# Weights split once, keys transposed before they are split: reordering the second half of a projection

## The chip, the cores and the metric

The kernel runs on one core of a Trainium2 chip. Its time is the device time of one execution in microseconds (us), as a median of several runs. TensorE is called PE here, ScalarE ACT, VectorE DVE, GpSimd POOL, and SP is the engine that issues most transfers.

## The reference, cut to what matters

The model is a two-layer encoder of width 1024 on one sequence of 1024 positions: one attention layer, one gated MLP layer, each followed by a dense MLP. Only the start of the first layer is touched by the change: the projection to queries, keys and values.

```python
def gqa_attention(h, w_qkv, q_g, k_g, w_o, cos, sin):
    qkv = h @ w_qkv                                   # 16 query heads, 4 key and 4 value heads of 64
    q, k, v = jnp.split(qkv, [Q_WIDTH, Q_WIDTH + KV_WIDTH], axis=-1)
    q = apply_rope(rmsnorm(q.reshape(B, T, N_HEADS, HEAD_DIM), q_g), cos, sin)
    k = apply_rope(rmsnorm(k.reshape(B, T, N_KV_HEADS, HEAD_DIM), k_g), cos, sin)
    ...
    s = jnp.einsum('bqkgd,bskd->bkgqs', q_blk, k).astype(jnp.float32) * scale
    p = jax.nn.softmax(s, axis=-1).astype(v.dtype)
    return jnp.einsum('bkgqs,bskd->bqkgd', p, v)
```

Everything is float32. The kernel multiplies at the faster rounded type (float32r) and keeps the precision by splitting operands into a rounded high part and the remainder: a product a·b becomes three matmuls, a_hi·b_hi + a_hi·b_lo + a_lo·b_hi. A split is an ACT cast (hi) and a subtraction on DVE or POOL (lo).

## The kernel before

The projection works on two halves of 512 positions. For each half, the normed and modulated input `hs` (second half: `hs1`) is split in 8 tiles of 128 channels. The weights have three column blocks of 512: block 0 holds all keys and values, block 1 the first eight query heads, block 2 the other eight. `qkv_mm(cb, kp, ps, hp)` (L573 to L582) multiplies block `cb` with channel pair `kp`, 24 matmuls into four PSUM banks, one for each 128 positions. A block of one half is four such calls, 96 matmuls.

Weights come through `qkv_w` (L551 to L571): a load of 512 KB into a tile of the tag `c`, two casts, two subtractions. The splits of blocks 0 and 1 stay in memory for both halves. Block 2 is split for the first half, and its tiles are given up; for the second half it is loaded and split again, into tiles of the tags `s` and `w` (`keep=True`).

What is done with the results, in rows of positions:

- `values` splits the values straight out of PSUM. `k_copies` and `q_copies` bring keys and queries from PSUM to memory on ACT.
- `q_sums`, `k_scale`: sums of squares for each head (ACT squares, DVE reduces), a reciprocal root by an ACT square root and one Newton step on DVE, and `qk_scale`, the product with it, on POOL (L654).
- `qk_rope` rotates with the tables (L638 to L641): two products and a sum, on DVE; for the third block of the first half the last sum is POOL's, and its input is read straight out of PSUM.
- `k_split` (L670 to L679) splits the finished keys; each row tile has the four key heads, each head twice side by side.
- `kstacks` (L681 to L689) turns them to channels by positions: for each key head and each of hi and lo, four PE transposes into a bank and one ACT copy into a tile of the tag `x`. A score matmul later takes such a stack, with the same 64 channels in both halves of the partitions, against a query stack with hi above lo.
- `q_stage` splits queries for the attention on POOL, `q_trans` transposes them on PE.

PSUM has eight banks. `banks(True)` gives the four of the pool `ps_s` (two tiles of two banks), `banks(False)` the four of the pool `p_x`; `bank_x` and `bank_s` take one bank-sized tile out of the one or the other. A new tile waits until the oldest one in its place has been read.

The order on each engine comes from a scheduler that works from the order of the code; instructions handed to `pin` or `hold` keep theirs. From the attention on almost all is pinned: its units follow a written order of stages, in which POOL and DVE get further work (`deferred`) at fixed places.

Of the kernel before, what the change touches and what calls it, by code (L numbers as in the profile page):

```python
# [12 lines left out]
F32R = mybir.dt.float32r  # L13
AF = mybir.ActivationFunctionType
ALU = mybir.AluOpType
# [3 lines left out]
P = 128  # L19
# [5 lines left out]
NKV = 4  # L25
HD = 64
EPS = 1e-6
CB = 512
# [8 lines left out]
def encoder_kernel(ctx: ExitStack, tc: tile.TileContext, t: dict, out: bass.AP):  # L37
    nc = tc.nc
    V, S, G, T = nc.vector, nc.scalar, nc.gpsimd, nc.tensor
# [35 lines left out]
    def cwide(dt=F32, shape=(1024,)):  # L75
        return part["pool"].tile([P] + list(shape), dt, tag="c", name=nm("c"), bufs=4)
# [466 lines left out]
    qn = {}  # L543
    kst = {}
# [3 lines left out]
    if True:  # L548
        wq = {}

        def qkv_w(cb, kp, eng, keep=False):  # L551
            raw = qkv_hi(cb, kp, keep)
            for i in range(2):
                qkv_lo(cb, kp, raw, i, eng)
# [14 lines left out]
        def qkv_lo(cb, kp, raw, i, eng):  # L569
            hi, lo = wq[(cb, 2 * kp + i)]  # L570
            hold(eng.tensor_tensor(lo, raw[:, i], f32(hi), ALU.subtract))  # L571

        def qkv_mm(cb, kp, ps, hp, part=(0, 1)):  # L573
            for i in part:
                k = 2 * kp + i
                wh, wl = wq[(cb, k)]
                for j in range(4):
                    hh = hp[k][0][:, j * P : (j + 1) * P]
                    hl = hp[k][1][:, j * P : (j + 1) * P]
                    hold(T.matmul(ps[j], hh, wh, start=k == 0, stop=False))  # L580
                    hold(T.matmul(ps[j], hh, wl, start=False, stop=False))
                    hold(T.matmul(ps[j], hl, wh, start=False, stop=k == KT - 1))  # L582
# [10 lines left out]
        def k_copies(ps):  # L593
            raws = []
            for jj in range(2):
                raw = slot()
                for i in range(2):
                    S.copy(raw[:, i * 256 : (i + 1) * 256], ps[2 * jj + i][:, :256])
                raws.append(raw)
            return raws  # L600

        def q_copies(ps):
            raws = []
            for j in range(4):
                raw = slot()
                S.copy(raw, ps[j])
                raws.append(raw)
            return raws

        def values(hf, ps):  # L610
            for j in range(4):
                v_ = slot(F32R)
                vv = v_.rearrange("p (g s d) -> p g s d", g=NKV, s=2)
                pv = ps[j][:, 256:].rearrange("p (g d) -> p g d", g=NKV)
                S.copy(vv[:, :, 0], pv)
                pin(V.tensor_tensor(vv[:, :, 1], pv, f32(vv[:, :, 0]), ALU.subtract))
# [32 lines left out]
        def q_sums(src):  # L649
            return qk_rstd(qk_sums(src))  # L650
# [5 lines left out]
        def q_rope(hf, cb, src, r, js, add=None):  # L656
            for j in js:
                d = qk_rope(src[j], 0, hf * 4 + j, 1, V, add)
                qk_scale(d, r, j)
                qn[(hf * 4 + j, cb - 1)] = d  # L660

        def k_rows(hf, src):
            return [qk_rope(src[j], 1, hf * 4 + 2 * j, 2) for j in range(2)]

        def k_scale(kd, src):
            r = qk_rstd(qk_sums(src))
            for j in range(2):
                qk_scale(kd[j], r, j)

        def k_split(kd):  # L670
            kk = []
            for j in range(4):
                kh, kl = slot(F32R), slot(F32R)
                src = heads(kd[j // 2], 2)[:, j % 2].unsqueeze(2).broadcast_to([P, NKV, 2, HD])
                hv = kh.rearrange("p (g s d) -> p g s d", g=NKV, s=2)
                S.copy(hv, src)
                V.tensor_tensor(kl.rearrange("p (g s d) -> p g s d", g=NKV, s=2), src, f32(hv), ALU.subtract)
                kk.append((kh, kl))
            return kk  # L679

        def kstacks(hf, kk, bank):  # L681
            for g in range(NKV):
                for s in range(2):
                    pt = bank("kt", dt=F32R)
                    for j in range(4):
                        T.transpose(pt[:, j * P : (j + 1) * P], kk[j][s][:, g * P : (g + 1) * P], identr)
                    d_ = xslot(F32R)
                    S.copy(d_, f32(pt))
                    kst[(g, hf, s)] = d_  # L689

        row = wide("c")
        nc.sync.dma_start(row[0:1, :], t["cond"])
# [1 line left out]
        xs = [load_x(0, k) for k in range(KT)]  # L694
# [14 lines left out]
        sq0, sq1 = SquareSum(), SquareSum()  # L709
# [17 lines left out]
        rb = slot()  # L727
        hs = []
# [60 lines left out]
        pk, pq = banks(True), banks(False)  # L789
# [5 lines left out]
            if k < 6:  # L795
                qkv_mm(1, k // 2, pq, hs, (k % 2,))
        xs1 = [load_x(1, k) for k in range(KT)]
        qkv_w(2, 0, V)
        values(0, pk)
        rk = k_copies(pk)  # L800
        qkv_mm(1, 3, pq, hs, (0,))
        qkv_w(2, 1, V)
        for k in range(2):
            sq1.add(xs1[k])
        tables(*raw_tables)
        qkv_mm(1, 3, pq, hs, (1,))
        ps = banks(True)
        qkv_mm(2, 0, ps, hs)
        r1 = q_copies(pq)
        qkv_w(2, 2, V)  # L810
        for k in range(2, 5):
            sq1.add(xs1[k])
        qkv_mm(2, 1, ps, hs)
        qkv_w(2, 3, V)
        for k in range(5, KT):
            sq1.add(xs1[k])
        qkv_mm(2, 2, ps, hs, (0,))
# [13 lines left out]
        rr2 = q_sums(ps)  # L831
        q_rope(0, 2, ps, rr2, (0, 1), G)
        qkv_mm(0, 1, pk, hs1)
        q_rope(0, 2, ps, rr2, (2, 3), G)
        qkv_mm(0, 2, pk, hs1)
        qkv_w(2, 0, V, True)
        kk = k_split(kd)
        qkv_mm(0, 3, pk, hs1)
        rk = k_copies(pk)
        values(1, pk)  # L840
        pq = banks(True)
        qkv_mm(1, 0, pq, hs1)
# [76 lines left out]


    with ExitStack() as es:

        def q_stage(qq, g):
            qh = []
            for j in range(2):
                q_ = qn[(2 * qq + j, g // 2)]
                src = q_[:, (g % 2) * 256 : (g % 2) * 256 + 256].rearrange("p (h d) -> p h d", h=4)
                d_ = slot(F32R)
                dv = d_.rearrange("p (h s d) -> p h s d", h=4, s=2)
                G.tensor_copy(dv[:, :, 0], src)  # L930
                G.tensor_tensor(dv[:, :, 1], src, f32(dv[:, :, 0]), ALU.subtract)
                qh.append(d_)
            return qh

        def q_trans(qh, hp, qst, bank=bank_x):
            pt = bank("qt", dt=F32R)
# [95 lines left out]
        r2 = q_copies(ps)  # L1032
        rr2 = {}
        r1, rr1 = list(r1), rr
# [18 lines left out]
        del hs, hs1, xs, xs1, rb, rb1, ps, pk, pq, rk, kk, kd, sq0, sq1, wq, r3  # L1053
        for i in range(nu + 2):
            u0 = units[i] if i < nu else None
            u1 = units[i - 1] if 0 < i <= nu else None
# [5 lines left out]
            for op in ORDER.split():  # L1062
                f, w, j = op[0], int(op[1]), int(op[2])
# [402 lines left out]
    for ct in range(24):  # L1466
        i, r = divmod(ct, 3)
# [404 lines left out]
```

## Time and profile before

| | |
|---|---|
| median of 3 runs | 2625.0 us (2622.57 to 2626.14) |
| profiled execution | 2625.42 us |
| its span, first to last instruction | 2623.6 us |
| mean granted TensorE clock | 0.997 |
| PE / DVE / ACT / POOL busy | 99% / 83% / 55% / 28% |
| projection | from the start to about 170 us |
| attention | about 155 to 550 us |
| time from one matmul's start to the next, 128x128 on 512 columns | 0.23 us (one is shown as 0.39: they overlap) |

A row of a timeline has the start, the duration, the engine, the line, the operation with output and inputs (buffer numbers left out), the shape, how many equal ones follow each other (x), and in brackets how long the engine was idle before it and which instruction ended that. Since matmuls overlap, the rate of PE is read from starts, not from durations.

### The profile page before, as it was taken

What the parts mean: (1) busy time and instruction counts of PE and PEld (TensorE: products, weight loads), DVE (VectorE), ACT (ScalarE), POOL (GpSimd) and SP (SyncE); (2) the same over time, 40 slices, a digit from 0 to 9 for tenths busy, and PEclk for the clock granted to TensorE, in tenths of its full rate; (3) what the DMA queues carried; (4) which work ended last, traced back from release to release, by engine and by line L of the source; (5) the groups of instructions that cost most, each with busy time, mean ns of one, the idle gap of its engine ahead of it and who ended that gap; (6) DMA issues with size and microseconds to landing.
All of it is one profiled execution on the core that took longest, in us unless ns stands there. A gap on an engine that the chain in (4) does not pass through costs nothing.

```text
span 2623.6 us, 37299 instructions
## 1 busy us (share of the span) xinstructions
PE 2595.9 (99%) x12856; PEld 2172.3 (83%) x12856; DVE 2185.8 (83%) x3285; ACT 1443.2 (55%) x2588; POOL 722.8 (28%) x531
## 2 busy tenths in 40 slices
PE   9999999999999999999999999999999999999999
PEld 7789999888788888888888888888888788888887
DVE  7868999887989989877897687788989977789974
ACT  4569998854654455445543444445456644465442
POOL 0238776533000004430122054451520000005400
PEclk9999999999999999999999999999999999999999
DMA  8010222234487788644243355568641554487461
GB/s 301 32 33 9 73 85 79 97 100 158 159 287 253 262 312 305 203 126 171 89 153 112 117 183 178 179 208 303 236 143 52 175 178 157 151 314 264 149 213 56
DMA packets 209328, 436.44 MB, mean 166 GB/s; under 512 B 23089, under 2 KB 35505, under 8 KB 209138
## 3 DMA queue, kind: packets, MB, share of 16 engines
q1 hardware_dynamic: 182258, 396.29, 44.8%
q10 hardware_dynamic: 26880, 37.76, 4.0%
q8 instruction: 102, 1.67, 0.3%
q14 instruction: 88, 0.72, 0.1%
HBM read 311.28 MB, written 122.68 MB: 165 GB/s over the span
## 4 chain that ended last, share of the span: by engine, by line
PE 86%; DVE 7%; DMA 3%; ACT 2%; issue 1%; POOL 1%; SPq 0%; DVEq 0%; ACTq 0%
PE w L474 10%; PE w L475 10%; PE w L476 10%; PE out L1218 10%; PE out L1219 10%; PE out L1217 10%; PE s L953 4%; PE o L989 4%; PE t L970 4%; PE v L1576 3%; PE v L1575 3%; PE v L1574 3%; PE mix L1681 2%; DVE t L334 1%; PE qkv L580 1%
## 5 line engine op out<-in xcount | busy, mean ns | idle before, releaser
L1217 PE MATMUL out<-t,s 128*128 128x512 f32 x1232 | 479.5, 390 | 1.2 <-ACT t L333 0.6
L1218 PE MATMUL out<-t,s 128*128 128x512 f32 x1232 | 479.6, 390 | 0.7 <-DVE t L334 0.7
L1219 PE MATMUL out<-t,s 128*128 128x512 f32 x1232 | 479.2, 389 | 0.0
L474 PE MATMUL w<-t,s 128*128 128x512 f32 x1168 | 458.7, 394 | 0.5 <-ACT t L333 0.5
L475 PE MATMUL w<-t,s 128*128 128x512 f32 x1168 | 455.5, 390 | 1.8 <-DVE t L334 1.8
L476 PE MATMUL w<-t,s 128*128 128x512 f32 x1168 | 454.9, 389 | 0.0
L334 DVE TENSOR_TENSOR t<-t,t 128x512 fp32r<-128x512 f32 x408 | 324.2, 805 | 24.4 <-ACT t L333 16.8
L333 ACT CAST t<-t 128x512 fp32r<-128x512 f32 x408 | 245.2, 617 | 120.3 <-DMA t<-hf 70.9
L1217 PEld LDWEIGHTS out<-t,s 128*128 128x128 f32 x1232 | 231.3, 188 | 50.2 <-ACT t L333 1.0
L1218 PEld LDWEIGHTS out<-t,s 128*128 128x128 f32 x1232 | 231.3, 188 | 49.6 <-DVE t L334 1.9
L1219 PEld LDWEIGHTS out<-t,s 128*128 128x128 f32 x1232 | 231.3, 188 | 47.7
L459 ACT CAST s<-w 128x512 fp32r<-128x512 f32 x292 | 173.4, 616 | 164.7 <-PE w L476 107.6
L475 PEld LDWEIGHTS w<-t,s 128*128 128x128 f32 x1168 | 219.5, 188 | 48.7 <-DVE t L334 5.2
L474 PEld LDWEIGHTS w<-t,s 128*128 128x128 f32 x1168 | 219.5, 188 | 47.8 <-issue 2.6
L460 DVE TENSOR_TENSOR s<-w,s 128x512 fp32r<-128x512 f32 x292 | 221.4, 765 | 44.1 <-ACT s L459 43.7
L476 PEld LDWEIGHTS w<-t,s 128*128 128x128 f32 x1168 | 219.4, 188 | 45.4
L1199 ACT CAST s<-t 128x512 fp32r<-128x512 f32 x240 | 148.2, 621 | 193.7 <-PE out L1219 140.2
L1200 DVE TENSOR_TENSOR s<-t,s 128x512 fp32r<-128x512 f32 x240 | 196.7, 821 | 63.1 <-ACT s L1199 62.3
L1185 POOL TENSOR_TENSOR w<-w,t 128x512 f32<-128x512 f32 x20 | 33.4, 1681 | 768.0 <-DMA t<-in_wm_dram 355.1
L956 DVE TENSOR_REDUCE mx<-s 128x1 f32<-128x1024 f32 x128 | 156.3, 1221 | 31.6 <-PE s L953 29.8
L979 DVE TENSOR_TENSOR t<-t,t 128x512 fp32r<-128x512 f32 x256 | 164.2, 682 | 17.8 <-ACT t L973 16.7
L989 PE MATMUL o<-t,t 128*128 128x256 f32 x1024 | 163.5, 293 | 0.0
(253 smaller groups left out, 5081.8 us busy)
## 6 DMA issues: line engine op xcount, KB each, us to landing
t<-hf SPq DMA_DIRECT2D x320, 256.0 KB, 4.1
hf<-c SPq DMA_DIRECT2D x156, 256.0 KB, 3.2
w<-in_wi_dram SPq DMA_DIRECT2D x64, 512.0 KB, 4.2
hf<-c ACTq DMA_DIRECT2D x96, 256.0 KB, 2.3
w<-in_ada_dram SPq DMA_DIRECT2D x36, 512.0 KB, 4.1
x<-in_ada_dram SPq DMA_DIRECT2D x64, 256.0 KB, 5.7
t<-in_wm_dram SPq DMA_DIRECT2D x64, 256.0 KB, 4.8
wf<-w SPq DMA_DIRECT2D x64, 256.0 KB, 2.9
```

What stands on the lines that cost most here:

```text
L333: S.copy(hi, src)
L334: (eng or V).tensor_tensor(lo, src, f32(hi), ALU.subtract)
L459: S.copy(hi, src)
L460: V.tensor_tensor(lo, src, f32(hi), ALU.subtract)
L474: T.matmul(ps, hi[:, a], th, start=kt == 0, stop=False)
L475: T.matmul(ps, hi[:, a], tl, start=False, stop=False)
L476: T.matmul(ps, lo[:, a], th, start=False, stop=kt == 3)
L989: pin(T.matmul(u.po, vt[st][:, u.g * P : (u.g + 1) * P], src[:, s * 256 : (s + 1) * 256], start=st == 0 and part == 0, stop=st == 7 and pa ...
L1200: V.tensor_tensor(lo, src, f32(hi), ALU.subtract)
L1217: T.matmul(ps, hi[:, a], th, start=begin and kt == 0, stop=False, **g)
L1218: T.matmul(ps, hi[:, a], tl, start=False, stop=False, **g)
L1219: T.matmul(ps, lo[:, a], th, start=False, stop=end and kt == 3, **g)
```

## The change

Five things are done, all within the projection.

1. The weights of block 2 are loaded and split once, by a new `qkv_w2`, in loads of 256 KB into tiles of the tag `x`; the high parts stay in tiles `t`, the low parts in tiles `c`, for both halves. The second calls of `qkv_w(2, ...)` are gone.
2. The first queries' copies (`r1`) go to tiles `x` in place of `t`. Third-block queries of the first half are copied out of PSUM by `q_copies` and rotated from there, all on DVE.
3. `k_split` is gone. `kstacks` transposes the scaled keys themselves, two heads at a time (16 transposes in place of 64), and splits them out of PSUM: an ACT cast of one head's 64 partitions, a DVE subtraction for the low part, and an ACT copy of each to the other 64 partitions.
4. The second half's key rows, sums and scale come straight after its key block, the key stacks earlier in the following block; the first key stacks use `bank_s`. The rotations of first and third query block change places.
5. `q_stage(0, 0)` stands in the projection, ahead of the last rotations.

```diff
+        def qkv_w2(kp):
+            lo = wide("c", F32R, (2, CB))
+            for i in range(2):
+                raw, hi = xslot(), slot(F32R)
+                nc.sync.dma_start(raw, t["wqkv"][2, kp][:, i])
+                hold(S.copy(hi, raw))
+                hold(V.tensor_tensor(lo[:, i], raw, f32(hi), ALU.subtract))
+                wq[(2, 2 * kp + i)] = (hi, lo[:, i])
...
-        def k_split(kd):
...
-        def kstacks(hf, kk, bank):
-            for g in range(NKV):
-                for s in range(2):
-                    pt = bank("kt", dt=F32R)
-                    for j in range(4):
-                        T.transpose(pt[:, j * P : (j + 1) * P], kk[j][s][:, g * P : (g + 1) * P], identr)
-                    d_ = xslot(F32R)
-                    S.copy(d_, f32(pt))
-                    kst[(g, hf, s)] = d_
+        def kstacks(hf, kd, bank):
+            for gp in range(2):
+                pt = bank("kt")
+                for j in range(4):
+                    src = kd[j // 2][:, (j % 2) * 256 + gp * P : (j % 2) * 256 + (gp + 1) * P]
+                    T.transpose(pt[:, j * P : (j + 1) * P], src, ident)
+                for i in range(2):
+                    a, b = 64 * i, 64 - 64 * i
+                    hi, lo = xslot(F32R), xslot(F32R)
+                    S.copy(hi[a : a + 64], pt[a : a + 64])
+                    V.tensor_tensor(lo[a : a + 64], pt[a : a + 64], f32(hi[a : a + 64]), ALU.subtract)
+                    S.copy(hi[b : b + 64], f32(hi[a : a + 64]))
+                    S.copy(lo[b : b + 64], f32(lo[a : a + 64]))
+                    kst[(2 * gp + i, hf, 0)], kst[(2 * gp + i, hf, 1)] = hi, lo
...
-        qkv_w(2, 0, V)
+        qkv_w2(0)
         values(0, pk)
         rk = k_copies(pk)
...
-        r1 = q_copies(pq)
-        qkv_w(2, 2, V)
+        r1 = q_copies(pq, xslot)
+        qkv_w2(2)
...
         pk = banks(False)
         qkv_mm(0, 0, pk, hs1)
-        rr2 = q_sums(ps)
-        q_rope(0, 2, ps, rr2, (0, 1), G)
+        r2 = q_copies(ps)
         qkv_mm(0, 1, pk, hs1)
-        q_rope(0, 2, ps, rr2, (2, 3), G)
+        kstacks(0, kd, bank_s)
+        q_rope(0, 1, r1, rr, (0, 1))
         qkv_mm(0, 2, pk, hs1)
-        qkv_w(2, 0, V, True)
-        kk = k_split(kd)
         qkv_mm(0, 3, pk, hs1)
         rk = k_copies(pk)
+        kd = k_rows(1, rk)
+        k_scale(kd, rk)
         values(1, pk)
         pq = banks(True)
         qkv_mm(1, 0, pq, hs1)
-        kd = k_rows(1, rk)
-        qkv_w(2, 1, V, True)
         qkv_mm(1, 1, pq, hs1)
-        kstacks(0, kk, bank_x)
-        k_scale(kd, rk)
-        kk = k_split(kd)
+        q_rope(0, 1, r1, rr, (2, 3))
         qkv_mm(1, 2, pq, hs1)
-        qkv_w(2, 2, V, True)
-        q_rope(0, 1, r1, rr, (0, 1))
+        kstacks(1, kd, bank_x)
+        qh = q_stage(0, 0)
+        rr2 = q_sums(r2)
         qkv_mm(1, 3, pq, hs1)
-        qkv_w(2, 3, V, True)
         r3 = q_copies(pq)
-        kstacks(1, kk, bank_x)
+        q_rope(0, 2, r2, rr2, (0, 1))
         ps = banks(False)
         qkv_mm(2, 0, ps, hs1)
-        q_rope(0, 1, r1, rr, (2, 3))
         rr = q_sums(r3)
+        q_rope(0, 2, r2, rr2, (2, 3))
...
-        qh = q_stage(0, 0)
         nxt = []
         q_trans(qh, 0, nxt, bank_s)
```

How this moves instructions is shown at three places. The first is PE, at the first half's key transposes (`kt`). Before they stood in the middle of the second half's first query block (`qkv_1114` is its last bank), 32 in a row:

```order
L580 MATMUL qkv_1114<-t_292,t_843 128x512
L581 MATMUL qkv_1114<-t_293,t_843 128x512
L582 MATMUL qkv_1114<-t_292,t_845 128x512
L686 MATMUL kt_1183<-identr,t_1055 128x128
L686 MATMUL kt_1183<-identr,t_1059 128x128
L686 MATMUL kt_1183<-identr,t_1063 128x128
L686 MATMUL kt_1183<-identr,t_1067 128x128
L686 MATMUL kt_1190<-identr,t_1056 128x128
```

Now (`t_782` and `t_788` are the key tiles as scaled by POOL, `qkv_925` to `qkv_928` the banks of the second half's key/value block):

```order
L589 MATMUL qkv_925<-w_379,t_859 128x512
L590 MATMUL qkv_925<-w_379,t_859 128x512
L591 MATMUL qkv_925<-w_379,t_861 128x512
L696 MATMUL kt_985<-ident,t_782 128x128 x2
L696 MATMUL kt_985<-ident,t_788 128x128 x2
L589 MATMUL qkv_926<-w_379,t_859 128x512
L590 MATMUL qkv_926<-w_379,t_859 128x512
L696 MATMUL kt_1002<-ident,t_782 128x128 x2
L696 MATMUL kt_1002<-ident,t_788 128x128 x2
L591 MATMUL qkv_926<-w_379,t_861 128x512
```

The eight transposes have moved up into the key/value block, between matmuls of its sixth channel tile (63 matmuls of the block stand ahead of them). Those of the second half have moved likewise, from behind the first query block to a place after 72 of its matmuls.

The second place is ACT at the second half's key stacks. Before, behind the copies of the first queries (`qkv_1113`, `qkv_1114`):

```order
L606 COPY t_1351<-qkv_1113 128x512
L606 COPY t_1353<-qkv_1113 128x512
L606 COPY t_1355<-qkv_1114 128x512
L606 COPY t_1357<-qkv_1114 128x512
L688 CAST x_1364<-kt_1359 128x512
L688 CAST x_1371<-kt_1366 128x512
L688 CAST x_1378<-kt_1373 128x512
L688 CAST x_1385<-kt_1380 128x512
```

Now (L700 is the cast out of PSUM, L702 and L703 the copies of the high and low part to the other partitions):

```order
L700 CAST x_1222<-kt_1217 64x512
L702 CAST x_1222<-x_1222 64x512
L703 CAST x_1223<-x_1223 64x512
L700 CAST x_1228<-kt_1217 64x512
L702 CAST x_1228<-x_1228 64x512
L700 CAST x_1239<-kt_1234 64x512
L703 CAST x_1229<-x_1229 64x512
L702 CAST x_1239<-x_1239 64x512
L703 CAST x_1240<-x_1240 64x512
L700 CAST x_1245<-kt_1234 64x512
L615 COPY t_1303<-qkv_1129 128x512
```

Two banks in place of eight are emptied, each by casts that stand between copies, and DVE's four subtractions (L701, `x_1223`, `x_1229`, `x_1240`, `x_1246`) alternate with them; the copies of the queries come behind. The second of these banks (`kt_1234`) is the one that the last query block's fourth tile, `qkv_1328`, takes over.

The third place is ACT at the first half's values and keys. Before (`qkv_222` and `qkv_223` are key/value tiles of two banks):

```order
L565 CAST t_586<-c_584 128x512
L565 CAST t_589<-c_584 128x512
L615 CAST t_594<-qkv_222 128x4x64
L615 CAST t_597<-qkv_222 128x4x64
L615 CAST t_600<-qkv_223 128x4x64
L615 CAST t_603<-qkv_223 128x4x64
L598 COPY t_606<-qkv_222 128x256 x2
L598 COPY t_609<-qkv_223 128x256 x2
```

Now:

```order
L578 CAST t_586<-x_585 128x512
L578 CAST t_591<-x_590 128x512
L624 CAST t_595<-qkv_222 128x4x64
L624 CAST t_598<-qkv_222 128x4x64
L624 CAST t_601<-qkv_223 128x4x64
L615 COPY x_687<-qkv_224 128x512
L615 COPY x_689<-qkv_225 128x512
L624 CAST t_604<-qkv_223 128x4x64
L607 COPY t_607<-qkv_222 128x256 x2
L615 COPY x_691<-qkv_226 128x512
L607 COPY t_610<-qkv_223 128x256 x2
```

Three copies of first queries (`qkv_224` to `qkv_226`) have moved up among the values' casts and the key copies.

From the attention's first scores on, the order of each engine is what it was.

More of the change, by code (lines that the diff above doesn't have):

```diff
@@ L600, in k_copies, with q_copies @@
             return raws
-        def q_copies(ps):
+        def q_copies(ps, home=slot):
             raws = []
             for j in range(4):
-                raw = slot()
+                raw = home()
                 S.copy(raw, ps[j])
@@ L668, in k_scale, with q_stage @@
                 qk_scale(kd[j], r, j)
-        def k_split(kd):
-            kk = []
-            for j in range(4):
[L673 to L679, printed above, removed]
-        def kstacks(hf, kk, bank):
-            for g in range(NKV):
-                for s in range(2):
-                    pt = bank("kt", dt=F32R)
-                    for j in range(4):
-                        T.transpose(pt[:, j * P : (j + 1) * P], kk[j][s][:, g * P : (g + 1) * P], identr)
-                    d_ = xslot(F32R)
-                    S.copy(d_, f32(pt))
-                    kst[(g, hf, s)] = d_
+        def q_stage(qq, g):
+            qh = []
+            for j in range(2):
+                q_ = qn[(2 * qq + j, g // 2)]
+                src = q_[:, (g % 2) * 256 : (g % 2) * 256 + 256].rearrange("p (h d) -> p h d", h=4)
+                d_ = slot(F32R)
+                dv = d_.rearrange("p (h s d) -> p h s d", h=4, s=2)
+                G.tensor_copy(dv[:, :, 0], src)
+                G.tensor_tensor(dv[:, :, 1], src, f32(dv[:, :, 0]), ALU.subtract)
+                qh.append(d_)
+            return qh
+        def kstacks(hf, kd, bank):
[12 more added lines that the diff above has]
+                    kst[(2 * gp + i, hf, 0)], kst[(2 * gp + i, hf, 1)] = hi, lo
         row = wide("c")
@@ L801, in encoder_kernel @@
         qkv_mm(1, 3, pq, hs, (0,))
-        qkv_w(2, 1, V)
+        qkv_w2(1)
         for k in range(2):
@@ L813, in encoder_kernel @@
         qkv_mm(2, 1, ps, hs)
-        qkv_w(2, 3, V)
+        qkv_w2(3)
         for k in range(5, KT):
@@ L921, in encoder_kernel @@
     with ExitStack() as es:
[L923 to L933, printed above, removed]
         def q_trans(qh, hp, qst, bank=bank_x):
@@ L1052, in encoder_kernel @@
             deferred[3 + 2 * j] = lambda j=j: late_rope(j)
-        del hs, hs1, xs, xs1, rb, rb1, ps, pk, pq, rk, kk, kd, sq0, sq1, wq, r3
+        del hs, hs1, xs, xs1, rb, rb1, ps, pk, pq, rk, kd, sq0, sq1, wq, r3
         for i in range(nu + 2):
```

## Prediction

> **What bounds the kernel now.** I read the page's busy times first, then the waits of the matrix engine (PE) in the stage that changes, then the timelines of PE, ScalarE (ACT), VectorE (DVE) and GpSimd (POOL) there.
>
> ```profile
> PE 2595.9 (99%) x12856; PEld 2172.3 (83%) x12856; DVE 2185.8 (83%) x3285; ACT 1443.2 (55%) x2588; POOL 722.8 (28%) x531
> ```
>
> PE is busy 99% of the span, so only two things shorten this kernel: fewer PE instructions, or fewer PE waits. Here is PE in the projection; columns are start, duration, instruction, and in brackets the idle time before it with what ended it.
>
> ```profile
> 66.83 0.50 PE L580 MATMUL qkv<-t,t 128*128 128x512 f32 x1 [0.85 <-ACT t L598]
> ...
> 89.69 0.39 PE L580 MATMUL qkv<-s,t 128*128 128x512 f32 x1
> ...
> 111.30 0.39 PE L582 MATMUL qkv<-w,t 128*128 128x512 f32 x1
> 113.80 0.47 PE L580 MATMUL qkv<-t,t 128*128 128x512 f32 x1 [2.11 <-DVE t L640]
> ...
> 124.58 0.39 PE L582 MATMUL qkv<-t,t 128*128 128x512 f32 x1
> 126.53 3.20 PE L686 MATMUL kt<-identr,t 128*128 128x128 f32 x32 [1.56 <-DVE t L616]
> ...
> 140.55 1.50 PE L686 MATMUL kt<-identr,t 128*128 128x128 f32 x16
> 142.37 2.01 PE L686 MATMUL kt<-identr,t 128*128 128x128 f32 x16 [0.32 <-ACT x L688]
> 144.33 0.50 PE L580 MATMUL qkv<-s,t 128*128 128x512 f32 x1
> ```
>
> At 89.69 us the second half's key/value block begins, at 113.80 its first query block, at 144.33 its second. The first block's 96 matmuls run without a wait, so one takes (111.30 − 89.69) / 95 = 0.2275 us. From 111.30 to 144.33 are 33.03 us, of which 97 matmuls are 22.07; the other 10.96 are 64 key transposes and the waits around them. After that the attention stage runs on PE alone, whatever starts it earlier:
>
> ```profile
> 225.00:250.00 25.00, 25.00 (x186) 23.14 (x186) 21.65 (x27) 23.46 (x47) 24.14 (x28) 1.00 0.00 1
> ```
>
> The columns after the length are PE, weight loads, DVE, ACT, POOL: PE has 25.00 of 25 us. From the first unit's scores on, PE's order is unchanged by the diff, so what is won before it should reach the end.
>
> **The change, part by part.**
>
> *Key transposes.* 64 become 16, now of plain f32 keys. The 16 at 140.55 take 1.50, 0.094 each. Transposes of plain f32 exist in the attention:
>
> ```profile
> 169.69 1.03 PE L970 MATMUL t<-ident,c 128*128 128x128 f32 x8
> 170.48 0.48 PE L953 MATMUL s<-x,t 128*128 128x512 f32 x1
> ```
>
> Eight in 0.79, 0.099 each: the type costs next to nothing, so 16 are 1.5 us. The Trainium skill ("TensorE: Matmul & The Clock Gate", Part 4: PE-mode transpose) gives about 275 ns for a transpose inside a kernel. By it 48 fewer would be worth 13.2 us, more than the 10.96 us that stand there for transposes and waits together; the rows decide.
>
> *The waits at 113.80, 126.53 and 142.37.* The first was for query rows rotated straight out of PSUM; now four ACT copies free those banks. The second was for values queued behind key splits and weight splits on DVE, both gone from there. The third was for ACT copying eight stacks out one by one. Without all three: 10.96 − 1.5 = **−9.5 us** before new waits.
>
> *Weights of the third block.* The second half's four loads, 8 casts and 8 subtractions go. PE waited for none of them, so by themselves they are worth nothing; they shorten queues, below. The first half's four loads become eight of half the size, in other buffers; the third and fourth pairs now wait for DVE's split of the first and second.
>
> ```profile
> DMA to landing us min/median/max: 3.3/7.0/9.7
> ```
>
> That covers all loads of these weights. The fourth pair can be issued at about 69 us, when the second is split; the DMA queues are then nearly empty, so I take the minimum, 72.3, before ACT reaches the cast. At the maximum, 78.7, the squares behind the cast would come some 2 us after PE's need of them at 66.83 + 60 × 0.2275 = 80.5. Taken as 0, bound +2.
>
> *New order on ACT at the first values.* Three copies of the first queries now stand among the values' casts, two of them ahead of the copies that free the bank PE waited for at 66.83.
>
> ```profile
> 62.33 1.14 ACT L565 CAST t<-c 128x512 fp32r<-128x512 f32 x2 [4.17 <-DMA c<-in_wqkv_dram]
> ...
> 64.65 0.65 ACT L615 CAST t<-qkv 128x256 fp32r<-128x256 f32 x2 [0.91 <-DVE t L616]
> 65.85 0.37 ACT L615 CAST t<-qkv 128x256 fp32r<-128x256 f32 x1 [0.55 <-DVE t L616]
> 66.12 1.24 ACT L598 COPY t<-qkv 128x256 f32<-128x256 f32 x4
> ...
> 69.34 2.04 ACT L606 COPY t<-qkv 128x512 f32<-128x512 f32 x4
> ```
>
> A copy costs 0.51; two are 1.02, less the 0.55 that ACT idled there: +0.5. Against it the cast at 62.33, which waited for a 512 KB load, can start on the first half, up to 0.6 earlier. I take **+0.2**, bounds −0.1 and +0.5.
>
> *ACT and DVE work of the key split.* Before: 8 casts, 16 copies and 8 subtractions. After: 8 casts, 16 half-tile copies, 8 subtractions. Half the partitions is no cheaper by the nearest row, which takes the 0.37 that the whole tile of that width took at 65.85:
>
> ```profile
> 179.97 0.37 ACT L999 COPY t<-o 64x256 f32<-64x256 f32 x1
> ```
>
> So for the split both engines do as much as before; only the order and the holding of banks change. The rotations of the third block lose POOL's part: four sums of 0.6 come to DVE, counted in its queue below.
>
> *Key scale, now in front of PE.* The first half's keys are transposed in the middle of the key/value block, after 63 of its matmuls: 89.69 + 63 × 0.2275 = 104.0. Two transposes later (104.2) PE needs the second key tile as POOL has scaled it. Before:
>
> ```profile
> 93.34 0.69 DVE L571 TENSOR_TENSOR s<-c,s 128x512 fp32r<-128x512 f32 x1
> ...
> 99.22 0.68 DVE L571 TENSOR_TENSOR s<-c,s 128x512 fp32r<-128x512 f32 x1
> ...
> 100.48 1.27 DVE L628 TENSOR_REDUCE qss<-t 128x8 f32<-128x512 f32 x2
> ```
>
> ```profile
> 99.30 2.70 ACT L627 ACTIVATE t<-t 128x512 f32<-128x512 f32 x5
> 102.02 1.28 ACT L245 ACT_TABLE_LOAD   x1
> ```
>
> ```profile
> 104.61 2.05 POOL L654 TENSOR_TENSOR t<-t,r 128x512 f32<-128x512 f32 x2 [21.06 <-ACT t L627]
> ```
>
> POOL was done at 106.66. Three weight splits of 0.6 (first and last shown) fall out of DVE here. Two of them stood ahead of the norm's last tile, which ACT's squares, table load and root follow, so that all shifts by 1.2, to 105.45, and PE waits **+1.2**. If the third counts too it is 0.6; if nothing shifts, 2.5.
>
> *Bank waits.* The first query block of the second half goes into the banks of these key transposes and begins at 89.69 + 96 × 0.2275 + 0.75 + 1.2 = 113.5, with the second bank at 114.9. ACT's 11 operations there (0.51 each, from 105.8, with two waits for DVE) and DVE's last subtraction free them at 112 to 113.5: no wait. The other half's transposes stand after 72 matmuls of that block, at 113.5 + 16.4 = 129.9, and the last query block needs the second of their banks 8 transposes and 33 matmuls later, at 138.1. ACT's ten operations up to the last cast take about 5.3 from 130.4, and a subtraction of 0.7 follows, so the bank is free at 136.5, if DVE is there in time. DVE's queue from 98.6 (100.48 less three splits) to there holds 12 reduces, six rotations, eight subtractions out of PSUM and four short chains for the norms. Prices:
>
> ```profile
> 145.51 0.68 DVE L638 TENSOR_TENSOR t<-t,t 128x512 f32<-128x512 f32 x1
> 146.11 0.68 DVE L641 TENSOR_TENSOR t<-t,t 128x512 f32<-128x512 f32 x1
> 146.71 1.60 DVE L640 TENSOR_TENSOR t<-t,t 128x256 f32<-128x256 f32 x2
> 148.34 0.69 DVE L641 TENSOR_TENSOR t<-t,t 128x512 f32<-128x512 f32 x1
> 148.95 2.46 DVE L628 TENSOR_REDUCE qss<-t 128x8 f32<-128x512 f32 x4
> ```
>
> ```profile
> 146.93 1.09 POOL L654 TENSOR_TENSOR t<-t,r 128x512 f32<-128x512 f32 x1 [1.97 <-DVE t L641]
> ```
>
> Reduces are 0.61 (7.3); a rotation is 0.6 + 0.7 + 0.6 (11.4); subtractions 0.35 to 0.6 (3.8); the chains an estimated 1.5 each (6), with the table load inside the first. The L640 pair beside POOL's operation took 1.60, where 512 columns in one piece take 0.68: each POOL operation costs DVE some 0.9. With four, 3.6. The sum is 32.1, so DVE arrives at 130.7, just in time. If all ten POOL operations there block it, it is 5.4 more, and PE waits some 3. I take **+0.4**, bounds 0 and 3.
>
> *Moved up.* The first queries' splits on POOL, which so far end just ahead of their transposes, now run behind the key scale, at about 127 to 130, and their transposes stand 48 matmuls into the last query block, near 147: covered by 17 us.
>
> **Sum:** −9.5 + 0.2 + 1.2 + 0.4 = −7.7 us. The profiled execution took 2625.4 (its span of 2623.6 and 1.8 around it) and so would take 2617.7; it lies 0.4 above the median of the runs, 2625.0, so the forecast is **2617.3**.
>
> **Rivals.**
>
> 1. *Both key chains come late.* The key split now alternates ACT and DVE on one bank, a cast and a subtraction twice over, 2 × (0.51 + 0.68) = 2.4 us, where before one copy of 0.51 emptied it. Waits of 2.5 at the first transposes, 2.1 at the last block's bank (inside its bound), 0.5 early: −9.5 + 5.1 = −4.4, 2620.6. For it: DVE arrives without slack in my count. Against: it needs DVE some 3 us behind that count. The Trainium skill ("PSUM — Partial Sum Buffer", PSUM bank collisions raise a hardware error) says that two engines may not touch one bank and quadrant at once, so that the two have to take turns. By that rule the 2.4 can't be overlapped; the trace agrees (ACT waited 0.91 and 0.55 for DVE on the value banks above).
> 2. *The attention swallows it*: its vector work, not PE, sets the pace, and an earlier start is waited out: 2625.0. Against: 25.00 of 25 above, and an order of work that does not depend on clock time.
> 3. *Slower.* The transposes stand mid-block on PE, so PE waits for POOL's scale however late it is. To be 5.25 us slower it would have to come 9.5 − 0.6 + 5.25 = 14.2 us after 104.2, at 118.4; even unmoved it comes at 106.7. Price at that point: 2630.3.
> 4. *No new waits at all*: 2625.0 − 9.5 = 2615.5.
>
> **Chances.** Forecast 0.61, late chains 0.22, swallowed 0.07, slower 0.04, no waits 0.06. A measurement tells 0.2% from no change, 5.25 us, so 2619.75 is the edge: forecast and no waits are faster, 0.67; late chains and swallowed the same, 0.29; slower 0.04. The forecast's own range is 2614.5 to 2619.7. The full range goes from no waits less 1 for the spread of runs, 2614.5, to late chains plus 1.4 for it, 2622.0.
>
> **What would show it.** In the new profile: 16 key transposes in four groups of four; no wait for a rotation before the first query block; a wait of about 1.2 inside the key/value block, released by POOL's scale; the second query block beginning near 136 in place of 144.3; the first scores 7 to 8 us earlier, and the attention's waits unchanged. Wrong it would be if the wait before the last query block's fourth bank is over 2 us, if the squares for the norm hold PE near 80, or if the first scores come 8 us earlier and the end does not.

## The result, and the profile after

The changed kernel takes 2613.8 us (median of 12 runs, 2610.45 to 2621.04); the kernel before took 2622.2 in 12 runs shared with it. The ratio is 0.9973, 95% interval 0.9963 to 0.9982: 7.1 us less (4.7 to 9.7), or 8.4 by the medians. Forecast was −7.7 us, and faster. The absolute number, 2617.3, came out 3.5 us too high, and the time lies 0.7 us under the range of 2614.5 to 2622.0.

The busy times of the page of after, and PE in the projection (start, duration, instruction, in brackets the idle time before it and what ended it):

```profile
PE 2593.0 (99%) x12808; PEld 2167.8 (83%) x12808; DVE 2179.8 (83%) x3281; ACT 1443.7 (55%) x2584; POOL 718.5 (27%) x527
```

```profile
85.78 0.60 PE L294 MATMUL rb<-ident,r 128*128 128x128 f32 x4
...
103.74 0.44 PE L696 MATMUL kt<-ident,t 128*128 128x128 f32 x2 [0.24 <-POOL t L663]
104.74 0.44 PE L696 MATMUL kt<-ident,t 128*128 128x128 f32 x2 [0.56 <-POOL t L663]
...
105.50 0.60 PE L696 MATMUL kt<-ident,t 128*128 128x128 f32 x4
...
113.00 0.39 PE L589 MATMUL qkv<-t,t 128*128 128x512 f32 x1
...
129.33 1.03 PE L696 MATMUL kt<-ident,t 128*128 128x128 f32 x8
...
135.69 0.39 PE L589 MATMUL qkv<-t,t 128*128 128x512 f32 x1
...
138.09 0.47 PE L589 MATMUL qkv<-t,t 128*128 128x512 f32 x1 [0.20 <-DVE x L701]
...
153.23 1.07 PE L952 MATMUL s<-x,t 128*128 128x512 f32 x4
```

Sixteen key transposes: two groups of four in the key/value block (the first of them broken by a wait) and eight in a row for the second half; two waits for POOL's scale, 0.8 us together; no wait before the first query block (113.00); the second query block at 135.69, where it stood at 144.33; 0.20 before its fourth bank. The waits of 2.11, 1.56 and 0.32 are gone. The first scores (the last row) begin at 153.23. POOL's first key scale, and the first and the last of DVE's subtractions out of the second half's key banks, in the same profile:

```profile
102.64 2.05 POOL L663 TENSOR_TENSOR t<-t,r 128x512 f32<-128x512 f32 x2 [19.79 <-ACT t L615]
```

```profile
131.78 0.68 DVE L701 TENSOR_TENSOR x<-kt,x 64x512 fp32r<-64x512 f32 x1
...
137.25 0.69 DVE L701 TENSOR_TENSOR x<-kt,x 64x512 fp32r<-64x512 f32 x1 [1.58 <-ACT x L700]
```

Single executions differ at the start: the first projection matmul came anywhere from 17.7 to 20.8 us in the profiles of this study. So I compare one stretch of PE's time that each profile has to itself: from the transposes that spread the second half's norm (`rb`, the first row above) to the first scores. The same two rows of the kernel before, and of a second profile of the changed kernel:

```profile
86.48 0.60 PE L294 MATMUL rb<-ident,r 128*128 128x128 f32 x4
161.52 1.07 PE L953 MATMUL s<-x,t 128*128 128x512 f32 x4
```

```profile
85.02 0.60 PE L294 MATMUL rb<-ident,r 128*128 128x128 f32 x4
...
152.42 0.84 PE L952 MATMUL s<-x,t 128*128 128x512 f32 x3
```

75.04 us before; 67.45 and 67.40 after: −7.6, twice the same.

### The profile page after: what moved, and what is told of

Same layout as the page of the kernel before. It is cut to its first block, busy times and chain, and to the rows that moved or that the text cites. A ratio compares the mean times of both kernels' runs of the same rounds, so it can differ in the third digit from the quotient of the medians.

```text
span 2618.8 us, 37177 instructions
## 1 busy us (share of the span) xinstructions
PE 2593.0 (99%) x12808; PEld 2167.8 (83%) x12808; DVE 2179.8 (83%) x3281; ACT 1443.7 (55%) x2584; POOL 718.5 (27%) x527
## 4 chain that ended last, share of the span: by engine, by line
PE 83%; DVE 9%; DMA 3%; ACT 3%; issue 1%; POOL 1%; SPq 0%; DVEq 0%; ACTq 0%; POOLq 0%
PE w L474 10%; PE w L475 10%; PE w L476 10%; PE out L1215 9%; PE out L1216 9%; PE out L1217 9%; PE s L952 4%; PE o L988 4%; PE t L969 4%; PE v L1574 3%; PE v L1573 3%; PE v L1572 3%; PE mix L1679 1%; DVE t L334 1%; DMA t<-hf 1%
```

## The experiments

Each was timed in 5 rounds beside the kernel before. "Stretch" is the one just described, in us, from one profile of each kernel; "waits" is the sum of PE's waits of 0.19 us or more inside it; "time" is the ratio to the kernel before, less 1, on 2621 us, with its interval.

| kernel | stretch | against before | waits in it | time |
|---|---|---|---|---|
| before | 75.0 | | 4.0 | |
| transposes alone | 70.6 | −4.4 | 4.4 | −1.3 (−3.7 to +1.0) |
| weights once alone | 77.9 | +2.8 | 4.9 | +1.8 (−0.5 to +3.9) |
| copied queries alone | 79.2 | +4.1 | 6.9 | +4.2 (+1.8 to +6.6) |
| weights and copies | 79.1 | +4.0 | 6.1 | +4.7 (+2.4 to +6.8) |
| copies, no sums on POOL | 78.6 | +3.5 | 4.8 | +2.1 (−0.3 to +4.5) |
| weights once, rotations first | 79.9 | +4.9 | 5.3 | +7.3 (+4.7 to +10.2) |
| the whole change, again | 67.4 | −7.6 | 1.0 | −7.1 (−9.7 to −4.5) |
| whole, 64 transposes | 71.5 | −3.6 | 0.2 | −3.9 (−6.3 to −1.6) |
| whole, 36 more matmuls | 75.6 | +0.5 | 1.0 | 0.0 (−2.4 to +2.4) |
| whole, stacks later | 68.8 | −6.2 | 1.9 | −5.0 (−7.3 to −2.4) |
| whole, weights split twice | 70.8 | −4.3 | 4.1 | −0.3 (−2.6 to +1.8) |
| whole, stacks held | 67.1 | −8.0 | 1.2 | −6.6 (−9.4 to −3.7) |

**Does an earlier start reach the end?**

> The changed kernel with 36 extra matmuls of 128x128 on 512 columns ahead of the second half's second query block (their result is overwritten by that block's first matmuls). Theory (PE sets the pace from there to the end): 36 x 0.2275 = 8.2 us later at the first scores, at the last scores and at the end; the time comes to that of the kernel before, within 1 us. Rival (the attention or a later stage waits out an earlier start): less than 4 us of the 8.2 are left at the end.

```diff
+        for k in range(3):
+            for j in range(4):
+                for w_ in wq[(2, k)] + wq[(2, k)][:1]:
+                    hold(T.matmul(ps[j], hs1[k][0][:, j * P : (j + 1) * P], w_, start=True, stop=True))
         qkv_mm(2, 0, ps, hs1)
```

The stretch grew by 8.2 us, as 36 matmuls should, and the median from 2615.2 (the changed kernel beside it) to 2621.0; the ratio to the kernel before is 1.0000 (0.9991 to 1.0009). So 5.9 of 8.2 by the medians and 7.1 by the ratios are found at the end, over the rival's bound of 4: most of what PE gets or loses here arrives there. Each ratio is uncertain by some 2.5 us, so a part of it may be lost on the way.

> The changed kernel once more, beside the two edits of it. Theory: -7.7 us against the kernel before (-6 to -9.7), and a profile in which the first scores, the last scores and the end are all about 8 us earlier than in the profile of before: the 3.5 us that the first profile of it gave back between 1500 and 1900 us are the spread of its runs, in the stage that weights from memory feed, and not the change. Rival (a stage late in the kernel takes back part of the lead because its transfers or helpers are bound to something else): the same 3 to 4 us are given back again at the same place, every time.

The first profile of the changed kernel ended only 4.8 us earlier than that of before though its scores began 8.3 earlier: PE had waited longer between 1500 and 1900 us. First that profile, then the second one of the same kernel; engine, line, what for, total, times, longest:

```profile
PE out L1215 <- ACT t L333: 2.2, 2, 2.0
PE w L474 <- DVE c L1683: 1.2, 1, 1.2
```

```profile
PE out L1215 <- ACT t L333: 0.6, 1, 0.6
```

The second span is 2612.7 against 2618.8. The lost 3.5 us belong to one execution; after its wait of 2.0 us the first profile also shows a granted clock of 0.66 from 1870 to 1875 us, where the second has 1.00. In attention, too, PE's waits did not grow (3.3 and 2.3 us on its two main reasons before, 3.4 and 1.8 after).

**What a transpose costs.**

> The changed kernel with each of the 16 key transposes done four times into the same place: 64 as before, nothing else changed. Theory: 48 x 0.094 = 4.5 us more than the changed kernel (4 to 5.5), the first scores later by the same amount. Rival (about 275 ns for a transpose in a kernel): 13.2 us more. Rival (transposes fill time in which PE would wait): 2 us or less.

```diff
-                    T.transpose(pt[:, j * P : (j + 1) * P], src, ident)
+                    for _ in range(4):
+                        T.transpose(pt[:, j * P : (j + 1) * P], src, ident)
```

The stretch grew by 4.1 us, while 0.8 us of waits that it had went (PE comes to the scaled keys later): 48 transposes took 4.9, 0.10 each; in time 3.1 by the ratios. The 275 ns that the Trainium skill gives ("TensorE: Matmul & The Clock Gate", Part 4: PE-mode transpose) would be 13.2.

> The kernel before, with the new way of making key stacks alone (16 transposes of the scaled keys, split out of PSUM) at the old places. Theory (a transpose is worth 0.094 us, and the chain that now splits out of a bank must be hidden): 48 x 0.094 = 4.5 us of PE work go and the 0.32 wait for ACT's copies goes, but the second half's stacks stand directly ahead of the second query block, which needs the third and fourth of the same banks 1.4 and 2.1 us later, while ACT and DVE take 3 to 5 us for each of the two: a new wait of 2 to 4 us there. The 1.56 us wait for values gets up to 1 shorter, since no split stands in front of them. Net -3 to -1 us, -0.04% to -0.11%. Rival (transposes are worth their price wherever they stand): -4.8 us. Rival (275 ns for a transpose): -13.

The edit takes the new `kstacks` alone into the kernel before, at the old two places. The stretch fell by 4.4, nearly the full price that the first rival named, against an expected 1 to 3. The waits' sum stayed, 4.4 against 4.0, but they are others:

```profile
113.05 0.47 PE L580 MATMUL qkv<-t,t 128*128 128x512 f32 x1 [2.11 <-ACT t L615]
...
124.05 1.03 PE L675 MATMUL kt<-ident,t 128*128 128x128 f32 x8
...
143.00 0.47 PE L580 MATMUL qkv<-s,t 128*128 128x512 f32 x1 [2.27 <-DVE x L680]
```

The first wait is as long as before, 2.11. The one for the values at the first stacks (1.56) fell away whole, since no key splits stand before them; a wait for a bank behind the split out of PSUM, 2.27, came as expected. The runs show only −1.3 (−3.7 to +1.0), which fits the expectation and not the stretch; this stays open (below).

**The waits, part by part.**

> The kernel before, with the third block's weights split once (first queries' copies in tiles x, as the whole change has it), nothing else. Theory (weights only shorten queues): three weight splits of 0.6 us leave VectorE ahead of the rotation that PE waits 2.11 us for, and four ahead of the values that PE waits 1.56 us for: the two waits together fall by 1.5 to 3 us; against it 0.2 at the first values. Net -1 to -3 us; the transposes still take 6 us. Rival (third-block loads hold PE or cost DMA time worth more): -4 us or more. Rival (loads in the first half come late, squares hold PE near 80 us): 0 to +2.

```diff
-        qkv_w(2, 0, V)
+        qkv_w2(0)
...
-        r1 = q_copies(pq)
+        r1 = q_copies(pq, xslot)
...
-        qkv_w(2, 0, V, True)
...
```

Not faster: +2.8 in the stretch, +1.8 (−0.5 to +3.9) in time. The two old waits did fall (to 0.9 and 0.3), but the first queries now sit in tiles `x`, which the key stacks need. ACT in that place:

```profile
139.14 2.60 ACT L697 CAST x<-kt 128x512 fp32r<-128x512 f32 x5
142.51 0.59 ACT L697 CAST x<-kt 128x512 fp32r<-128x512 f32 x1 [0.77 <-DVE t L649]
145.24 0.59 ACT L697 CAST x<-kt 128x512 fp32r<-128x512 f32 x1 [2.14 <-DVE t L649]
```

The last stack copies wait for DVE's rotations (L649) of those queries, and PE for the copies, 3.7 us in all. With the waits 0.9 us longer in sum, most of the rest of the +2.8 is a slower clock (last section).

> The kernel before with the third block's weights split once and the first queries' rotations moved ahead (first two tiles before the key block's last part, two after three parts of the first query block). Stretch from the norm's transposes to the first scores: 75.0 before, 77.9 with the weights alone, where ACT's last two stack copies waited for tiles x that the first queries held until VectorE had rotated them. Theory (the buffers couple the two): the waits for ACT at the stacks (1.7 and 2.0) go; the rotations fill VectorE's idle stretches ahead of the values and may cost 0 to 2 there: 74 to 76. Rival (the late stacks have another cause): 77 to 79.

The rotations of the first queries go ahead of the key block's last quarter and of the first query block's. As expected the wait for the stacks went (to 0.2), but the price was 4.2, not 0 to 2: the rotations now stand ahead of the values on DVE.

```profile
112.47 0.47 PE L589 MATMUL qkv<-t,t 128*128 128x512 f32 x1 [0.85 <-DVE t L649]
...
128.76 0.89 PE L695 MATMUL kt<-identr,t 128*128 128x128 f32 x8 [4.22 <-DVE t L625]
```

So the cause of the late stacks is shown, and also that moving the rotations alone only moves the wait.

> The kernel before, with the third-block queries of the first half copied out of PSUM by ACT and then rotated from there, nothing else. Theory: the 2.11 us wait before the first query block of the second half goes; VectorE's queue is as long as before, so the 1.56 us wait for values stays as it is or grows by up to 0.5, since PE arrives there 2 us earlier: it may grow by the whole 2 us, and then nothing is won before the 32 transposes. I take half: -1 us (-2.1 to 0). Rival (the waits are independent): -2.1 exactly, with the wait for the values at 1.56.

```diff
-        rr2 = q_sums(ps)
-        q_rope(0, 2, ps, rr2, (0, 1), G)
+        r2 = q_copies(ps)
+        rr2 = q_sums(r2)
+        q_rope(0, 2, r2, rr2, (0, 1), G)
...
```

The 2.11 us wait went, and the wait for the values rose from 1.56 to 6.53, which neither the theory nor its rival had. DVE's rotations of the last two tiles, first before, then with the copies (the last row is a later rotation, beside which POOL is idle); columns as above:

```profile
114.18 0.74 DVE L640 TENSOR_TENSOR t<-qkv,t 128x256 f32<-128x256 f32 x2
114.84 0.67 DVE L638 TENSOR_TENSOR t<-qkv,t 128x512 f32<-128x512 f32 x1
115.44 0.74 DVE L640 TENSOR_TENSOR t<-qkv,t 128x256 f32<-128x256 f32 x2
```

```profile
113.28 2.69 DVE L640 TENSOR_TENSOR t<-t,t 128x256 f32<-128x256 f32 x2
115.89 0.68 DVE L638 TENSOR_TENSOR t<-t,t 128x512 f32<-128x512 f32 x1
116.50 2.69 DVE L640 TENSOR_TENSOR t<-t,t 128x256 f32<-128x256 f32 x2
...
128.39 0.74 DVE L640 TENSOR_TENSOR t<-t,t 128x256 f32<-128x256 f32 x2
```

In both kernels POOL works at sums and scales beside the rotations of these two tiles. There a product that reads one operand from PSUM (`qkv`) takes 0.37; the same with both in memory takes 1.35. With POOL idle that one takes 0.37 too. The copies moved the rotations from the first kind to the second.

> The kernel before with the third-block queries copied out and the sums of their rotations on VectorE instead of GpSimd. The stretch from the transposes that spread the second half's norm to the first scores took 75.0 us before and 79.2 with the copies alone. Theory (VectorE's products of two operands in memory take 1.35 us in place of 0.37 beside a GpSimd operation, those with one operand in PSUM do not): the two slow pairs (2.69 against 0.74), a slow product (1.53 against 0.68) and a slow small one go, some 5 us, and four sums of 0.6 come: VectorE is at the values 2.4 us earlier, the 6.5 us wait for them falls to about 4, the stretch to 76.8 (76 to 78): still not under the 75.0. Rival (the copies make VectorE late, not GpSimd): four sums more on VectorE, 81.6.

Only the argument `G` is dropped, so the sums go to DVE; POOL's scales stay beside the rotations. The pairs fell to 1.60, and the wait for the values to 2.9, below the expected 4. That part of the theory holds, and DVE with four sums more was not later, as the rival had it. But the stretch came out at 78.6, not 76.8: at the second stacks PE, 4 us earlier there, waited 1.9 for ACT, and its clock fell (0.67 from 125 to 130 us, 0.50 from 145 to 150; see the last section).

> Both of the two before together, still with 64 transposes of split keys. Theory: both waits of PE (2.11 and 1.56 us) go nearly whole, since the copies free the banks and VectorE's queue is four splits shorter ahead of the values: -3 to -4 us, +0.2 at the first values. Rival (the gain of the whole change comes from the transposes alone): 0 to -1.

Wrong: +4.0 in the stretch and +4.7 in time, in place of −3 to −4. The waits for values (3.4) and stacks (1.7 and 1.0) are those of the two parts, shortened by each other.

**The other side: taking parts out of the whole.**

> The changed kernel with the third block's weights loaded and split a second time for the second half, at the old places. Stretch from the norm's transposes to the first scores: 67.4 in both profiles of the changed kernel. Theory (splitting once matters through VectorE's queue): three splits of 0.6 stand again ahead of the first key scale, so that PE waits 1.2 to 1.9 us more at the first key transposes, and four stand ahead of the second stacks' splits, where VectorE has no slack: up to 2.4 more at the last query block's banks. Stretch 69 to 72, time +1.5 to +4.5 us against the changed kernel. Rival (weights cost nothing where PE does not wait for them, as with that part alone): 67.4, +0.

The stretch is 70.8, inside the theory's 69 to 72: the second splits cost 3.4 us, and not nothing. The time rose by more, 6.8 us by the ratios against an expected 1.5 to 4.5; half of that the stretch does not explain. And the places were only half right: the transposes' wait for the scale stayed near where it was (0.56), since the scheduler put them seven instructions later on PE; DVE's late splits out of PSUM held both query blocks' banks, 1.2 and 2.4:

```profile
115.81 0.47 PE L589 MATMUL qkv<-t,t 128*128 128x512 f32 x1 [1.19 <-DVE x L701]
```

> The changed kernel with the first half's key stacks 12 matmuls (2.7 us) later in the key/value block. Theory: PE's 0.8 us of waits for POOL's scale at these transposes go; the banks of the first query block, which come free 2.7 us later, are needed no earlier than about 2 us after: a wait of 0 to 1.5 takes their place. Net -0.8 to +0.7 us against the changed kernel: not to be told by the time, but by the rows of the waits. Rival (the wait for the scale only moves, since VectorE's chain follows PE's pace): 0.8 again at the same transposes.

The call of `kstacks` stood 12 matmuls later in the code, but the scheduler left the transposes of the first stacks where they were in PE's order; only DVE's and ACT's work around them moved. The wait for the scale was 0.8 again, for that reason; 0.57 came at a bank of the first query block, and the wait at the last block's bank grew from 0.20 to 0.56. It tells nothing of the question.

> The changed kernel with the key transposes held in the written order, the first ones 9 matmuls (2.0 us) later on PE (the scheduler had put them as early as it thought the keys to be ready). Theory: GpSimd's scale is done 1.9 us after PE's arrival at the first transposes, so both waits for it (0.2 and 0.6) go; the banks are needed 2 us sooner after them, a wait of 0 to 1. Stretch 66.6 to 67.6; the time cannot tell it. Rival (the wait follows PE's pace): 0.8 again.

Here the call stands behind the whole third part of the block (24 matmuls), and the transposes are held in that order, 9 matmuls later on PE than in the change. All eight run in one go:

```profile
103.84 1.03 PE L696 MATMUL kt<-ident,t 128*128 128x128 f32 x8
...
113.07 0.47 PE L589 MATMUL qkv<-t,t 128*128 128x512 f32 x1 [1.15 <-DVE x L701]
```

No wait for the scale; 1.15 at the bank behind it, slightly over the expected bound. The stretch is 67.1, 0.3 less than the change's, which the time (median 2612.5) can't tell. The work is the same; the wait changed its place.

## Why the prediction was right in the gain and off in the level, point by point

- *Transposes, −4.5*: shown. 4.4 alone, 4.1 with 0.8 of waits given up when put back.
- *Three waits of PE gone, 4.0 us*: they went, but the causes that I gave one by one do not hold one by one. Copies alone do not remove a wait: they save 2.1 us there and make the wait for the values 5.0 longer. Weights split once leave a wait for tiles `x`. The parts in the old order sum to −4.4 + 4.0 = −0.4; the whole is −7.6. The other 7.2 us must come from what I had costed only as queue and bank terms: the new order (keys scaled and transposed early, first queries rotated ahead of the second stacks) and the rotations' sums off POOL. Two runs agree: with copied queries, weights split once and 64 transposes, the stretch is 79.1 in the old order and 71.5 in the new, 7.6 less, of which some 2 are the slower clock of the former. How much each piece of the new order is worth, no run separates. The prediction counted the work in the final order, so its sum came out; as an account of what each edit is worth it was wrong.
- *Gross −9.5*: −9.2. The stretch is 7.6 us shorter net of the new waits, which cost 1.6 by PE's starts (POOL's scale and the bank, below): 7.6 + 1.6.
- *Weights off DVE*: "by themselves worth nothing; they shorten queues". Split twice in the new order they cost 3.4 us in the stretch, through the queues.
- *DMA and ACT at the first values, +0.2*: the wait was 0.68 and 0.62 in place of 0.85, so −0.2; the added copies cost PE nothing there. ACT did wait 1.33 and 1.05 us for two later loads, the last of them issued at 72.3, where I had the last pair at about 69; the squares were done at 79.11, 0.75 ahead of PE's need of them at 79.86. So nothing was lost, but with little room.
- *POOL's scale, +1.2*: 0.8 of idle time, 1.2 by the starts: from 103.12 to 103.74 is 0.39 over one matmul's pace (the matmul ahead began at 103.12), and from there to 104.74 is 0.81 over two transposes'. POOL began at 102.64 in place of 104.61, 1.3 earlier once the start's 0.7 is taken off, as worked out.
- *Bank of the last query block, +0.4*: 0.20 of idle time, 0.36 by the starts. But the room was less than I had counted: DVE began that split at 131.78, forecast 130.7, and was done at 137.94, forecast 136.5, in an execution whose stretch began 0.7 earlier. Between the four subtractions DVE waited 3.4 us in all for ACT, whose copies to the other partitions stand between its casts.
- *Carried to the end*: shown for most of it by 36 matmuls, 5.9 or 7.1 of 8.2 us.
- *The level, 2617.3*: the mis-sized term is the start of the sum. The median of three runs, 2625.0, was high: 12 runs gave 2622.2, and later sets of 26 to 33 gave 2620.5 to 2621.4. From 2622.2 the same −7.7 gives 2614.5.

The rivals: both chains late (2620.6) did not come, the waits it priced at 2.5 and 2.1 were 0.8 and 0.2 (1.2 and 0.36 by the starts). Swallowed by attention did not come, and neither did slower by the transposes that it named. But parts of the change were slower in another way: the copied queries alone, and with the weights once, ended 4.2 and 4.7 us later, by a wait in front of PE that took the place of the one removed, and by a slower clock behind it. That the two pairs of cast and subtraction on a key bank can't overlap, as the first rival argued, no run shows. The waits of 0.91 and 0.55 that the prediction counts as agreement were for DVE on the other bank of the same two-bank tile. The two heads of a key bank lie on different partitions, and it was the order on ACT that kept the second cast back: the copy ahead of it waited 0.57 us for DVE, at 132.49.

Left open: for the transposes alone and for the weights split twice, the runs lie 3 to 4 us above what the stretch says. Both have waits of 2.3 us or so in it without a slow clock in their profiles; that other executions have one there (next section) would fit and is not shown.

## What to carry to other kernels

On a kernel whose matrix engine is 99% busy, count its instructions and its waits in the final order of work: the removed instructions arrive in PE's time near their price, while a removed wait is won only if the next queue behind it has room. Before copying an operand out of PSUM to free a bank, look who reads it next and what runs on POOL at that time. To compare versions 0.3% apart, measure a stretch between two marks of the changed stage in each profile; whole executions differ by more.

## What the runs showed of the hardware

**A short wait can cost half the clock afterwards.** Five of the kernels, the parts whose stretch grew, have 1.2 to 3.6 us more in the stretch than their waits explain, against the kernel before. Their granted clock says where. Windows of the kernel with the copied queries (wait of 6.53 up to 126.9) and of the one with the weights once (wait of 1.76 up to 145.9, and another of 1.75 up to 139.8); the column behind POOL's busy time is the clock:

```profile
125.00:130.00 5.00, 3.07 (x24) 3.08 (x25) 5.00 (x12) 2.29 (x5) 0.00 (x0) 0.51 0.00 0
```

```profile
140.00:145.00 5.00, 3.91 (x21) 2.54 (x20) 5.00 (x8) 2.33 (x5) 2.46 (x2) 1.00 0.00 0
145.00:150.00 5.00, 4.12 (x11) 3.33 (x12) 4.09 (x9) 2.90 (x6) 3.98 (x8) 0.66 0.00 0
150.00:155.00 5.00, 5.00 (x24) 4.14 (x23) 1.42 (x3) 0.00 (x0) 1.22 (x2) 1.00 0.00 0
```

A mean of 0.66 over 5 us is 3.4 us at half speed, so 1.7 us lost, on top of the wait of 1.76. The kernel before shows none after its 2.11 and 1.56:

```profile
110.00:115.00 5.00, 2.89 (x13) 2.12 (x12) 5.00 (x16) 2.41 (x5) 2.81 (x3) 1.00 0.01 2
115.00:120.00 5.00, 5.00 (x23) 4.13 (x22) 5.00 (x6) 1.39 (x5) 4.84 (x5) 1.00 0.00 0
...
125.00:130.00 5.00, 3.48 (x34) 3.28 (x35) 5.00 (x12) 3.24 (x8) 0.00 (x0) 1.00 0.00 0
130.00:135.00 5.00, 5.00 (x24) 4.12 (x23) 3.54 (x10) 2.35 (x6) 0.53 (x1) 1.00 0.02 3
```

So a wait of about 2 us sometimes costs 1.7 more. The length of the wait alone does not decide it. In the kernel with the weights once and the rotations first, the clock also falls within a row of 32 transposes (143.3 to 148.6 us), with no wait near it longer than 0.24:

```profile
145.00:150.00 5.00, 4.54 (x28) 3.83 (x28) 4.96 (x10) 4.38 (x9) 1.43 (x1) 0.66 0.00 0
```

What decides it stays open. The Trainium skill ("TensorE: Matmul & The Clock Gate", Part 1: The HAM clock gate) has the half rate after an idle window of some 3.4 us that runs free of the program; the length of the slow stretch agrees, but a wait of half a window, 1.76 us, was enough here.

**An operand in PSUM keeps DVE clear of POOL**: beside POOL 0.37 against 1.35 for the same product, and 0.37 for the second kind too with POOL idle, above. The Trainium skill ("SBUF — State Buffer", Who interferes with whom) says that a DVE instruction with at most one input in SBUF does not contend with GpSimd, and one with two does, with a GpSimd instruction that reads SBUF; these rows agree.
